# Feed-forward output product of a two-layer trunk on one core: 14 of 22 row blocks taken in pairs as 2x2 blocks with seven block products

## The chip, the cores and the metric

The kernel is one program on one core of a Trainium2 chip. The metric is the device time of one execution in microseconds (us). The engines named below are PE (the matrix engine), DVE (vector), ACT (scalar), POOL (general) and SP (which only issues DMAs here); each runs its own instructions in the order in which they stand in its queue and waits for semaphores of the others.

## The reference

Two layers; each has an attention part, a residual with layer norm, and a feed-forward part with the same residual and norm. SEQ is 512, D_MODEL 1024, D_FF 2816. The part that changes is the last matmul of `conv_ffn`:

```python
def conv_ffn(x, w_in, conv_w, conv_b, w_out):
    a, b = jnp.split(x @ w_in, 2, axis=-1)
    a = sum(conv_w[k] * a_pad[:, k:k + S] for k in range(CONV_W)) + conv_b
    return (jax.nn.gelu(a) * b) @ w_out
...
    ffn = conv_ffn(x, ffn_w_in[layer], ffn_conv_w[layer], ffn_conv_b[layer], ffn_w_out[layer])
    x = layer_norm(ALPHA * x + ffn, ln2_g[layer], ln2_b[layer])
```

All values are float32. The kernel holds each float32 operand as a high part `hi` (rounded by ACT to a narrower format that PE takes at full rate, fp32r) and a low part `lo` (the rest, by DVE), and makes each product as three matmuls: hi times hi, hi times lo, lo times hi.

## The kernel before

`layer0`, `ffn(0)`, `layer1`, `ffn(1)` run one after the other. The kernel's writer gives the instructions in program order; a list scheduler with a time model of its own then sets the order on each engine, so the order in the queues is not that of the source. Tiles come from pools with a fixed number of buffers: `raw` 5 (weights as loaded, 128x512), `hi` and `lo` 4 each (128x1024), `kj` 4 (128x1024), `kl` 2, `p` 4, `qq` 5 (128x512); a new tile of a pool waits until the last reader of a buffer is through.

The feed-forward part works on 22 blocks `f` of 128 hidden channels. Its input product makes, for each `f`, two sums `pa` (PSUM bank of tag `S`) and `pb` (tag `mm`), each 24 matmuls of 128x512 (`projT`: 8 slices of the model width by 3), with weights that `wab` loads, splits on ACT (L114) and DVE (L145) and hands over in `hi` and `lo`. `gate` (L592 to L598) applies the three-tap convolution and the gelu and writes `h[f]` (128 channels by 512 positions), by two ACT and three DVE instructions.

The output product sums over `f` into eight PSUM banks at once: four row tiles of 128 positions (`tb`) by two column halves of 512. `prep` splits `h[f]` into a `kj` tile and loads and splits the row block of `w_out`; `acc` then makes 4 x 2 x 3 = 24 matmuls of 128x512. So 528 matmuls a layer. The last blocks (TAIL: 5 in layer 0, 6 in layer 1) are all prepared first and then taken row tile by row tile, so that the first row tile's norm (`affine`, L540 to L565, mostly DVE) runs beside the products of the next. Each bank is added to the residual `nat[tb]` by one DVE instruction (L655). In layer 0 the norm is followed by transposes (L128) into the next layer's `xh`, `xl`; the memory keys and values of layer 1 (`mem_kv`) are placed there to fill PE.

## Time and profile before

| | us |
|---|---|
| median of 3 runs | 1282.38 (1282.27 to 1283.21) |
| span of the profiled execution | 1278.2 |
| median less that span | 4.2 |
| PE busy in the span | 1231.1 (96%) |
| DVE busy | 726.7 (57%) |
| ACT busy | 596.5 (47%) |
| POOL busy | 275.7 (22%) |

For the profiled execution the profile has the span, from its first instruction to its last, and no time of its own beside it; the runs' median lies 4.2 us above the span. A row of a group gives line, engine, operation, output from inputs, shape and count, then busy us, mean ns of one, and the idle time before it with what ended it. A row of the timeline gives start us, length us, engine, line, operation, shape and count. Matmuls are pipelined: the length of one (0.39 us) is longer than the distance between two starts. A line can be that of a helper: every matmul of the products stands at L120, and tiles tell them apart.

### The profile page before, as it was taken

How to read it: one execution, taken by the hardware profiler on the slowest of the kernel's cores; microseconds unless marked ns; L12 is line 12 of the kernel's file. 1: busy time of each engine (PE TensorE's matmuls, PEld its weight loads, DVE VectorE, ACT ScalarE, POOL GpSimd, SP SyncE). 2: the span in 40 equal slices, each digit the busy share in tenths (PEclk: the TensorE clock that was granted, in tenths of full speed). 3: DMA queues.
4: the chain of work that ended last, by engine and by line, in shares of the span. 5: the costliest groups of instructions: out<-in, count | busy, mean ns of one | idle time of the engine just before them, and what ended most of it. 6: DMA issues, size and time to landing. Idle time of an engine off the chain costs nothing.

```text
span 1278.2 us, 18386 instructions
## 1 busy us (share of the span) xinstructions
PE 1231.1 (96%) x6400; PEld 1048.4 (82%) x6400; DVE 726.7 (57%) x1605; ACT 596.5 (47%) x1271; POOL 275.7 (22%) x364
## 2 busy tenths in 40 slices
PE   7899999989999999999998999998999999999996
PEld 6788888879888888888888898886988888888885
DVE  5457787898544444433385665558854444443347
...
GB/s 230 218 201 75 42 34 58 48 127 83 120 95 99 99 99 99 98 89 95 131 42 124 67 78 89 74 100 140 35 131 99 99 92 93 97 99 99 99 74 66
DMA packets 164724, 125.94 MB, mean 99 GB/s; under 512 B 10743, under 2 KB 141175, under 8 KB 164632
## 3 DMA queue, kind: packets, MB, share of 16 engines
...
q14 instruction: 41, 0.34, 0.1%
...
## 4 chain that ended last, share of the span: by engine, by line
PE 82%; DVE 10%; DMA 3%; ACT 2%; issue 1%; POOL 0%; SPq 0%; DVEq 0%; ACTq 0%; POOLq 0%
PE psmm L120 40%; PE psS L120 27%; PE psPT L120 7%; PE psO L120 5%; PE psPT L128 3%; DVE pt L117 1%; DMA kj<-in_mem_dram 1%; DVE st L521 1%; DVE p L295 1%; DVE nat L553 1%; DVE nat L560 1%; DVE nat L505 1%; ACT p L300 1%; DVE xl L117 1%; ACT pt L114 1%
## 5 line engine op out<-in xcount | busy, mean ns | idle before, releaser
L114 ACT ACTIVATE hi<-raw 128x512 fp32r<-128x512 f32 x370 | 213.5, 622 | 274.2 <-PE psS L120 181.3
L145 DVE TENSOR_TENSOR lo<-raw,hi 128x512 fp32r<-128x512 f32 x294 | 192.0, 692 | 188.6 <-ACT hi L114 187.1
L120 PE MATMUL psmm<-xh,hi 128*128 128x512 f32 (+1 forms) x560 | 212.1, 379 | 0.0
L120 PE MATMUL psmm<-xh,lo 128*128 128x512 f32 (+1 forms) x560 | 211.9, 378 | 0.0
L120 PE MATMUL psmm<-xl,hi 128*128 128x512 f32 (+1 forms) x560 | 211.8, 378 | 0.0
L145 POOL TENSOR_TENSOR lo<-raw,hi 128x512 fp32r<-128x512 f32 x76 | 99.3, 1330 | 399.8 <-ACT hi L114 398.3
L120 PE MATMUL psS<-xh,hi 128*128 128x512 f32 (+1 forms) x408 | 151.3, 371 | 0.9 <-ACT G L750 0.9
L120 PE MATMUL psS<-xl,hi 128*128 128x512 f32 (+1 forms) x408 | 151.5, 371 | 0.1
L120 PE MATMUL psS<-xh,lo 128*128 128x512 f32 (+1 forms) x408 | 150.9, 370 | 0.0
L120 PE MATMUL psmm<-hi,kj 128*128 128x512 f32 x392 | 137.3, 400 | 4.2 <-ACT kj L114 3.2
L120 PEld LDWEIGHTS psmm<-xh,lo 128*128 128x128 f32 x560 | 105.5, 188 | 18.9
L120 PEld LDWEIGHTS psmm<-xh,hi 128*128 128x128 f32 x560 | 105.4, 188 | 18.8 <-DVE qq L248 0.2
L120 PEld LDWEIGHTS psmm<-xl,hi 128*128 128x128 f32 x560 | 105.3, 188 | 18.8
L551 POOL TENSOR_TENSOR nat<-nat,p 128x384 f32<-128x384 f32 (+2 forms) x16 | 20.5, 1283 | 360.9 <-issue 329.5
L304 POOL TENSOR_SCALAR p<-p,s 128x128 f32<-128x128 f32 (+3 forms) x144 | 74.7, 536 | 96.4 <-DVE s L271 49.1
L300 ACT ACTIVATE p<-p,s 128x128 f32<-128x128 f32 (+3 forms) x144 | 79.9, 556 | 33.0 <-DVE s L295 32.2
L120 PEld LDWEIGHTS psmm<-hi,kj 128*128 128x128 f32 x392 | 73.7, 189 | 19.4 <-ACT kj L114 3.5
L120 PEld LDWEIGHTS psS<-xh,hi 128*128 128x128 f32 x408 | 77.5, 190 | 14.0 <-ACT G L750 1.0
L120 PEld LDWEIGHTS psS<-xl,hi 128*128 128x128 f32 x408 | 77.4, 190 | 13.3 <-DVE xl L117 0.3
L120 PEld LDWEIGHTS psS<-xh,lo 128*128 128x128 f32 x408 | 77.4, 190 | 12.8
L120 PE MATMUL psPT<-hi,kj 128*128 128x512 f32 x228 | 81.7, 389 | 0.0
L295 DVE CUSTOM_DVE_ANT_0 p<-psS,T 128x128 f32<-128x128 f32 (+3 forms) x144 | 66.1, 484 | 23.1 <-PE psS L120 19.9
...
## 6 DMA issues: line engine op xcount, KB each, us to landing
raw<-in_ffn_w_in_dram SPq DMA_DIRECT2D x176, 256.0 KB, 3.1
raw<-in_ffn_w_out_dram SPq DMA_DIRECT2D x88, 256.0 KB, 3.0
...
raw<-in_shared_w_kv_dram SPq DMA_DIRECT2D x24, 256.0 KB, 3.0
raw<-in_a_w_out_dram SPq DMA_DIRECT2D x16, 256.0 KB, 2.9
raw<-in_b_w_in_dram SPq DMA_DIRECT2D x16, 256.0 KB, 3.1
raw<-in_b_w_out_dram SPq DMA_DIRECT2D x16, 256.0 KB, 3.2
raw<-in_a_w_in_dram SPq DMA_DIRECT2D x14, 256.0 KB, 3.9
```

The costliest lines, as they stand in the source:

```text
L114: self.nc.scalar.activation(dst, src, AF.Copy)
L117: self.nc.vector.tensor_sub(dst, src, hi.bitcast(F))
L120: self.nc.tensor.matmul(o, l, r, start=start, stop=stop)
L128: self.nc.tensor.transpose(o, i, self.ident)
L145: eng.tensor_sub(l[:, c], raw, h[:, c].bitcast(F))
L295: nc.vector.tensor_tensor_reduce(L[i], dst[i], T[:, 384 - 128 * i:512], op0=ALU.add, op1=ALU.min, scale=1.0, scalar=BIG, accum_out=nm[:, i ...
L300: nc.scalar.activation(L[i], L[i], AF.Exp, bias=nm[:, i:i + 1], scale=-1.0, accum_out=sm[:, i:i + 1])
L304: nc.gpsimd.tensor_scalar(L[i], L[i], r[:, i - qs[0]:i - qs[0] + 1], 1.0, op0=ALU.mult, op1=ALU.mult)
L505: nc.vector.scalar_tensor_tensor(self.nat[tb][:, sl], self.nat[tb][:, sl], ALPHA if first else 1.0, ps, op0=ALU.mult, op1=ALU.add)
L521: nc.vector.bn_stats(st[:, 6 * j:6 * j + 6], x[:, c0:c1])
L551: nc.gpsimd.tensor_mul(x[:, p], x[:, p], gt[:, p])
L553: nc.vector.scalar_tensor_tensor(x[:, d], x[:, d], mu, gt[:, d], op0=ALU.subtract, op1=ALU.mult)
```

## The change

Fourteen of the 22 blocks are taken in seven pairs. With the pair's two channel blocks split into position halves (a, c of the first; b, d of the second) and the two weight rows into column halves (v11, v12; v21, v22), the four output quarters need eight block products. The change makes seven of them, each 2 x 3 = 6 matmuls of 128x512 into two banks:

- `first`, made during the input product, while `pa` and `pb` of the other blocks go on: a times v11 into two banks `A`, and (c-a-d) times (v11+v12+v22) into two banks `B6`. `prepare` loads the four weight quarters into `raw`, makes the sums of weights on DVE and keeps them in tiles of `kj`, `p`, `kl`, `T`, `pc`, `ot` and `pt` that the input product does not use; it also overwrites the halves of `h` by their differences.
- `take_first`, once at the end of the input product: u = A + B6, added to or taken from six quarters of `nat`, which is scaled by ALPHA there.
- `second`: (a-c) times (v12+v22) into two banks `B7` (tag `S`), (c-d) times (v11+v12) into two banks `C5` (tag `mm`). No DMA; splits of 128x1024 and 128x512.
- `take_second`: four DVE instructions (L159) add B7 and C5 to `nat`. The banks then go on as part of the sums.
- `third`: b times v21 into `A`, (c-a-d+b) times v22 into `C5`, d times (v11+v12+v22+v21) into `B7`. The row of v21, v22 is loaded and split a second time. Two `kj` tiles per pair.

The other eight blocks go the old way, two or three of them between the pairs of `third`; the tail is as before. Per pair 42 matmuls take the place of 48. In the two programs PE has 5794 matmuls by the helper `mm` before and 5710 after, DVE 206 instructions more, ACT 74 more, SP 28 DMAs more.

```diff
--- before.py
+++ after.py
@@ -56,11 +56,125 @@
-YB = (("PT", "PT"), ("mm", "mm"), ("S", "S"), ("PT", "O"))
+NPAIR = 7
+KEEP_W = ("kj", "p", "p", "p", "p", "kl", "kl")
+KEEP_W4 = ("T", "T", "pc", "pc", "ot", "pt", "pt")
 HALVES = ((0, 512), (512, D))
+class Blocks:
+    def __init__(self, t, h, w):
+        self.t, self.h, self.w, self.k = t, h, w, {}
+        self.A = self.B6 = None
+    def raw(self, f, half):
+        r = self.t.al("raw")
+        self.t.nc.sync.dma_start(r, self.w[128 * f:128 * f + 128, 512 * half:512 * half + 512])
+        return r
+    def prepare(self, i):
+        t, nc = self.t, self.t.nc
+        h1, h2 = self.h[2 * i], self.h[2 * i + 1]
+        a, c, b, d = h1[:, 0:256], h1[:, 256:512], h2[:, 0:256], h2[:, 256:512]
+        ws = t.al(KEEP_W[i])
+        if KEEP_W[i] == "p":
+            s4 = ws[:, 1024:1280]
+        else:
+            if "s" not in self.k:
+                self.k["s"] = [t.al("kj"), 0]
+            n = self.k["s"][1]
+            s4 = self.k["s"][0][:, 256 * n:256 * n + 256]
+            self.k["s"][1] += 1
+        w4 = t.al(KEEP_W4[i])
+        v11, v12, v22, v21 = self.raw(2 * i, 0), self.raw(2 * i, 1), self.raw(2 * i + 1, 1), self.raw(2 * i + 1, 0)
+        w1, w3 = ws[:, 0:512], ws[:, 512:1024]
+        wh, wl = t.al("hi", R), t.al("lo", R)
+        t.hi(wh[:, 0:512], v11)
+        t.lo(wl[:, 0:512], v11, wh[:, 0:512])
+        nc.vector.tensor_add(w1, v11, v12)
+        nc.vector.tensor_add(w3, v12, v22)
+        nc.vector.tensor_add(w4, w1, v22)
+        t.hi(wh[:, 512:1024], w4)
+        t.lo(wl[:, 512:1024], w4, wh[:, 512:1024])
+        nc.vector.tensor_add(w4, w4, v21)
+        g = t.al("kj", R)
+        t.hi(g[:, 0:256], a)
+        t.lo(g[:, 512:768], a, g[:, 0:256])
+        nc.vector.tensor_sub(a, a, c)
+        nc.vector.scalar_tensor_tensor(s4, a, -1.0, d, op0=ALU.mult, op1=ALU.subtract)
+        nc.vector.tensor_sub(c, c, d)
+        t.hi(g[:, 256:512], s4)
+        t.lo(g[:, 768:1024], s4, g[:, 256:512])
+        nc.vector.tensor_add(s4, s4, b)
+        self.k[i] = ws, s4, w4
+        return g, wh, wl
+    def product(self, banks, lh, ll, rh, rl, start, stop, more=False):
+        for j in range(2):
+            c = slice(128 * j, 128 * j + 128)
+            self.t.mm3(banks[j], lh[:, c], ll[:, c], rh, rl, start, stop, more)
+    def first(self, i, e):
+        g, wh, wl = e
+        if self.A is None:
+            self.A, self.B6 = [self.t.ps("PT"), self.t.ps("PT")], [self.t.ps("PT"), self.t.ps("O")]
+        x = i == 0, i == NPAIR - 1
+        self.product(self.A, g[:, 0:256], g[:, 512:768], wh[:, 0:512], wl[:, 0:512], *x)
+        self.product(self.B6, g[:, 256:512], g[:, 768:1024], wh[:, 512:1024], wl[:, 512:1024], *x)
+    def take_first(self):
+        t, nc = self.t, self.t.nc
+        self.C5, self.B7 = [t.ps("mm"), t.ps("mm")], [t.ps("S"), t.ps("S")]
+        self.y = [[self.A[0], self.C5[0]], [self.A[1], self.C5[1]], [self.B7[0], self.B6[0]], [self.B7[1], self.B6[1]]]
+        for j in range(2):
+            u = t.al("qq")
+            nc.scalar.activation(u, self.A[j], AF.Copy)
+            nc.vector.tensor_add(u, u, self.B6[j])
+            for tb, c0, op in ((j, 512, ALU.subtract), (2 + j, 0, ALU.add), (2 + j, 512, ALU.subtract)):
+                x = t.nat[tb][:, c0:c0 + 512]
+                nc.vector.scalar_tensor_tensor(x, x, ALPHA, u, op0=ALU.mult, op1=op)
+    def second(self, i):
+        t = self.t
+        ws, h1 = self.k[i][0], self.h[2 * i]
+        g, wh, wl = t.al("kj", R), t.al("hi", R), t.al("lo", R)
+        t.hi(g[:, 0:512], h1)
+        t.lo(g[:, 512:1024], h1, g[:, 0:512])
+        t.hi(wh, ws[:, 0:1024])
+        t.lo(wl, ws[:, 0:1024], wh)
+        x = i == 0, i == NPAIR - 1
+        self.product(self.B7, g[:, 0:256], g[:, 512:768], wh[:, 512:1024], wl[:, 512:1024], *x)
+        self.product(self.C5, g[:, 256:512], g[:, 768:1024], wh[:, 0:512], wl[:, 0:512], *x)
+    def take_second(self):
+        for bank, op in ((self.B7, ALU.subtract), (self.C5, ALU.add)):
+            for j in range(2):
+                x = self.t.nat[2 + j][:, 512:1024]
+                self.t.nc.vector.tensor_tensor(x, x, bank[j], op=op)
+    def third(self, i):
+        t = self.t
+        _, s4, w4 = self.k[i]
+        h2 = self.h[2 * i + 1]
+        g = t.al("kj", R)
+        t.hi(g[:, 0:512], h2)
+        t.lo(g[:, 512:1024], h2, g[:, 0:512])
+        v = t.rows(self.w, 256 * i + 128)
+        q = t.al("qq", R)
+        t.hi(q[:, 0:256], s4)
+        t.lo(q[:, 256:512], s4, q[:, 0:256])
+        w = t.al("kj", R)
+        t.hi(w[:, 0:512], w4)
+        t.lo(w[:, 512:1024], w4, w[:, 0:512])
+        self.product(self.A, g[:, 0:256], g[:, 512:768], v[0][:, 0:512], v[1][:, 0:512], False, False, True)
+        self.product(self.C5, q[:, 0:256], q[:, 256:512], v[0][:, 512:1024], v[1][:, 512:1024], False, False, True)
+        self.product(self.B7, g[:, 256:512], g[:, 768:1024], w[:, 0:512], w[:, 512:1024], False, False, True)
 class Trunk:
@@ -116,13 +230,13 @@
-    def mm(self, o, l, r, start, stop):
-        self.nc.tensor.matmul(o, l, r, start=start, stop=stop)
-    def mm3(self, o, lh, ll, rh, rl, start, stop):
-        self.mm(o, lh, rh, start, False)
-        self.mm(o, lh, rl, False, False)
-        self.mm(o, ll, rh, False, stop)
+    def mm(self, o, l, r, start, stop, more=False):
+        self.nc.tensor.matmul(o, l, r, start=start, stop=stop, skip_group_check=more)
+    def mm3(self, o, lh, ll, rh, rl, start, stop, more=False):
+        self.mm(o, lh, rh, start, False, more)
+        self.mm(o, lh, rl, False, False, more)
+        self.mm(o, ll, rh, False, stop, more)
@@ -602,6 +716,7 @@
         w = [wab(f) for f in range(2)]
         self.los = (nc.vector,)
+        blocks = Blocks(self, h, wout)
         p = [(self.ps("S"), self.ps("mm")) for f in range(2)]
@@ -611,15 +726,20 @@
             gate(f, *p[f])
         for f in range(2, NF):
             wa, wb = wab(f)
+            pair = f // 2 - 1 if f % 2 == 0 and f // 2 - 1 < NPAIR else None
+            if pair is not None:
+                e = blocks.prepare(pair)
             pa, pb = self.ps("S"), self.ps("mm")
             self.projT(pa, wa)
             self.projT(pb, wb)
             gate(f, pa, pb)
-        gt, bt = self.gb(a["ln2_g"], a["ln2_b"], l)
-        y = [[self.ps(t) for t in ts] for ts in YB]
-        if not last:
-            self.new_xT()
+            if pair is not None:
+                blocks.first(pair, e)
+        blocks.take_first()
+        for i in range(NPAIR):
+            blocks.second(i)
+        blocks.take_second()
+        y = blocks.y
         def prep(f, store=None, tag="kj"):
             t = self.al(tag, R)
@@ -631,14 +751,27 @@
             sl = slice(128 * tb, 128 * tb + 128)
             for c0, c1 in cols:
                 c = slice(c0, c1)
+                own = tb >= 2 and c0 == 512
                 self.mm3(y[tb][c0 // 512][:, c0 % 512:c0 % 512 + c1 - c0], hh[:, sl], hl[:, sl], w[0][:, c], w[1][:, c],
-                         f == 0, f == NF - 1)
+                         f == 2 * NPAIR and own, f == NF - 1, not own)
         TAIL, nx, nv = (6, 4, 0) if last else (5, 0, 2)
-        for f in range(NF - TAIL):
+        plain = list(range(2 * NPAIR, NF - TAIL))
+        for i in range(NPAIR):
+            blocks.third(i)
+            if plain and i % 2 == 1:
+                f = plain.pop(0)
+                e = prep(f)
+                for tb in range(NT):
+                    acc(f, tb, *e)
+        for f in plain:
             e = prep(f)
-            for tb in (1, 0, 2, 3) if f == 0 else range(NT):
+            for tb in range(NT):
                 acc(f, tb, *e)
+        gt, bt = self.gb(a["ln2_g"], a["ln2_b"], l)
+        if not last:
+            self.new_xT()
+        TAIL, nx, nv = (6, 4, 0) if last else (5, 0, 2)
         stores = [None] * (TAIL - nv - nx)
@@ -652,7 +785,7 @@
                 for f in range(NF - TAIL, NF):
                     acc(f, tb, *es[f - NF + TAIL], ((c0, c1),))
                 c = slice(c0, c1)
-                nc.vector.scalar_tensor_tensor(self.nat[tb][:, c], self.nat[tb][:, c], ALPHA,
+                nc.vector.scalar_tensor_tensor(self.nat[tb][:, c], self.nat[tb][:, c], ALPHA if tb < 2 and c0 == 0 else 1.0,
                                                y[tb][c0 // 512][:, c0 % 512:c0 % 512 + c1 - c0], op0=ALU.mult, op1=ALU.add)
```

Where it moves instructions, the rows of the queues show it. The first place is DVE at the end of layer 0's input product. Before: `psS_5615` and `psmm_5616` are the two sums of the last block, `lo_...` are splits of the output weights.

```order
L145 TENSOR_TENSOR lo_5763<-raw_5764,hi_5762 128x512
L145 TENSOR_TENSOR lo_5763<-raw_5768,hi_5762 128x512
L593 SCALAR_TENSOR_TENSOR qq_5665<-psS_5615,cw,qq_5665 128x511
L595 SCALAR_TENSOR_TENSOR qq_5665<-psS_5615,cw,qq_5665 128x510
L598 TENSOR_TENSOR pt_3902<-qq_5665,psmm_5616 128x512
L145 TENSOR_TENSOR lo_5800<-raw_5801,hi_5799 128x512
L145 TENSOR_TENSOR lo_5800<-raw_5805,hi_5799 128x512
L117 TENSOR_TENSOR kl_6366<-pt_3902,kl_6366 128x512
L117 TENSOR_TENSOR kj_5833<-o_3896,kj_5833 128x512
L145 TENSOR_TENSOR lo_5837<-raw_5838,hi_5836 128x512
```

After: `psS_5907` and `psmm_5908` are the two sums of the last block, `psPT_4259` and `psO_4260` the banks of B6, `qq_5967` and `qq_5973` hold u, `nat_129` to `nat_132` are the four row tiles, `lo_6038` is the split of a kept weight sum of the fourth pair.

```order
L707 SCALAR_TENSOR_TENSOR qq_5957<-psS_5907,cw,qq_5957 128x511
L138 TENSOR_TENSOR qq_5967<-qq_5967,psPT_4259 128x512
L138 TENSOR_TENSOR qq_5973<-qq_5973,psO_4260 128x512
L231 TENSOR_TENSOR qq_6129<-kj_4172,qq_6129 128x256
L709 SCALAR_TENSOR_TENSOR qq_5957<-psS_5907,cw,qq_5957 128x510
L231 TENSOR_TENSOR qq_6166<-p_4369,qq_6166 128x256
L141 SCALAR_TENSOR_TENSOR nat_129<-nat_129,qq_5967 128x512
L141 SCALAR_TENSOR_TENSOR nat_131<-nat_131,qq_5967 128x512 x2
L141 SCALAR_TENSOR_TENSOR nat_130<-nat_130,qq_5973 128x512
L141 SCALAR_TENSOR_TENSOR nat_132<-nat_132,qq_5973 128x512 x2
L231 TENSOR_TENSOR lo_6038<-p_4755,hi_6037 128x1024
L712 TENSOR_TENSOR pt_3902<-qq_5957,psmm_5908 128x512
```

Between the two convolution steps and the product of the last gate stand now the additions of `take_first` and one wide split; before, the three of the gate stood together.

The second place is PE in the output product of layer 0. Before, the end of the second block (`kj_5722` is its split channel block) is like every other: three matmuls a bank, bank after bank.

```order
L120 MATMUL psS_5679<-hi_5725,kj_5722 128x512
L120 MATMUL psS_5679<-lo_5726,kj_5722 128x512
L120 MATMUL psS_5679<-hi_5725,kj_5722 128x512
L120 MATMUL psS_5680<-hi_5725,kj_5722 128x512
L120 MATMUL psS_5680<-lo_5726,kj_5722 128x512
L120 MATMUL psS_5680<-hi_5725,kj_5722 128x512
L120 MATMUL psPT_5681<-hi_5725,kj_5722 128x512
L120 MATMUL psPT_5681<-lo_5726,kj_5722 128x512
L120 MATMUL psPT_5681<-hi_5725,kj_5722 128x512
L120 MATMUL psO_5682<-hi_5725,kj_5722 128x512
```

After, at the start of `third`: `kj_6116` and `kj_6153` are the channel blocks of the first two pairs, `kj_6132` the summed weights of the first, `psPT_4257` and `psPT_4258` the banks A, `psS_5965` and `psS_5966` the banks B7, `psmm_5963` one of C5.

```order
L234 MATMUL psPT_4258<-hi_6119,kj_6116 128x512
L234 MATMUL psPT_4257<-hi_6156,kj_6153 128x512
L234 MATMUL psPT_4257<-lo_6157,kj_6153 128x512
L234 MATMUL psPT_4258<-hi_6156,kj_6153 128x512
L234 MATMUL psPT_4258<-lo_6157,kj_6153 128x512
L234 MATMUL psS_5965<-kj_6132,kj_6116 128x512 x3
L234 MATMUL psS_5966<-kj_6132,kj_6116 128x512 x3
L234 MATMUL psPT_4257<-hi_6156,kj_6153 128x512
L234 MATMUL psPT_4258<-hi_6156,kj_6153 128x512
L234 MATMUL psmm_5963<-hi_6119,qq_6129 128x512
```

The scheduler has mixed the products of neighbouring pairs, and the bank of C5 comes only after 18 matmuls of other banks.

The third place is DVE at the end of layer 0, in the norm of the last row tile (`nat_132`); `kj_...` are splits of the memory keys and values, `xl_...` of the next layer's input. Before:

```order
L531 TENSOR_SCALAR s_1252_6833<-s_1252_6833 128x1
L533 SCALAR_TENSOR_TENSOR s_1253_6834<-s_1252_6833,s_1254_6835 128x1
L534 SCALAR_TENSOR_TENSOR s_1253_6834<-s_1253_6834 128x1
L145 TENSOR_TENSOR lo_6995<-raw_6996,hi_6994 128x512
L535 SCALAR_TENSOR_TENSOR s_1252_6833<-s_1253_6834,s_1252_6833 128x1
L145 TENSOR_TENSOR lo_6995<-raw_7000,hi_6994 128x512
L536 SCALAR_TENSOR_TENSOR s_1253_6834<-s_1252_6833,s_1254_6835 128x1
L117 TENSOR_TENSOR kj_6571<-psmm_6592,kj_6571 128x4x64
L537 SCALAR_TENSOR_TENSOR s_1252_6833<-s_1253_6834,s_1252_6833 128x1
L560 SCALAR_TENSOR_TENSOR nat_132<-nat_132,s_1252_6833,p_5672 128x512
L560 SCALAR_TENSOR_TENSOR nat_132<-nat_132,s_1252_6833,p_5672 128x128
L117 TENSOR_TENSOR kj_6571<-psmm_6592,kj_6571 128x4x64
```

After:

```order
L645 TENSOR_SCALAR s_1318_7011<-s_1318_7011 128x1
L231 TENSOR_TENSOR kj_6740<-psmm_6715,kj_6740 64x256
L647 SCALAR_TENSOR_TENSOR s_1319_7012<-s_1318_7011,s_1320_7013 128x1
L648 SCALAR_TENSOR_TENSOR s_1319_7012<-s_1319_7012 128x1
L649 SCALAR_TENSOR_TENSOR s_1318_7011<-s_1319_7012,s_1318_7011 128x1
L650 SCALAR_TENSOR_TENSOR s_1319_7012<-s_1318_7011,s_1320_7013 128x1
L651 SCALAR_TENSOR_TENSOR s_1318_7011<-s_1319_7012,s_1318_7011 128x1
L674 SCALAR_TENSOR_TENSOR nat_132<-nat_132,s_1318_7011,p_6487 128x512
L674 SCALAR_TENSOR_TENSOR nat_132<-nat_132,s_1318_7011,p_6487 128x128
L231 TENSOR_TENSOR kj_6740<-psmm_6715,kj_6740 64x256
L231 TENSOR_TENSOR xl_6491<-psPT_6962,xh_6490 128x4x128
L259 TENSOR_TENSOR lo_7055<-raw_7056,hi_7054 128x512
```

Before, two weight splits (`lo_6995`) stand between the steps of the reciprocal root (L533 to L537) and ahead of the last step of the norm (L560), for which the last transposes wait. After, that chain (L647 to L651, then L674) stands together but for one small split, and the next weight split (`lo_7055`) stands behind it.

## The prediction

> **What bounds the kernel now.** The first view is the page: PE is busy for nearly the whole span, and the chain that ended last is PE for 82% of it.
>
> ```profile
> PE 1231.1 (96%) x6400; PEld 1048.4 (82%) x6400; DVE 726.7 (57%) x1605; ACT 596.5 (47%) x1271; POOL 275.7 (22%) x364
> PE 82%; DVE 10%; DMA 3%; ACT 2%; issue 1%; POOL 0%; SPq 0%; DVEq 0%; ACTq 0%; POOLq 0%
> ```
>
> The share is an average, so the feed-forward stretches are read by themselves, in the view of windows: input product and output product of layer 0, then of layer 1. The columns after the stretch are its length, then busy us of PE, weight load, DVE, ACT, POOL, the granted clock, the DMA share and GB/s.
>
> ```profile
> 460.00:520.00 60.00, 60.00 (x266) 49.70 (x265) 25.30 (x39) 19.83 (x33) 0.00 (x0) 1.00 0.33 98
> 560.00:600.00 40.00, 40.00 (x178) 33.14 (x177) 13.91 (x23) 13.04 (x24) 0.00 (x0) 1.00 0.30 95
> 1000.00:1060.00 60.00, 60.00 (x266) 49.70 (x265) 25.68 (x39) 20.39 (x34) 0.00 (x0) 1.00 0.34 99
> 1160.00:1200.00 40.00, 40.00 (x178) 33.10 (x178) 14.97 (x24) 12.97 (x24) 0.00 (x0) 1.00 0.30 93
> ```
>
> In all four PE never stops and its clock is whole; DVE is busy for 35 to 43%, ACT for 32 to 34%, POOL not at all. So here a matmul less is its distance less, as long as DVE and ACT keep up. The distance is in the timeline: one start in the input product and the start 48 matmuls later, then the same in the output product, 24 matmuls apart.
>
> ```profile
> 500.58 0.39 PE L120 MATMUL psmm<-xh,hi 128*128 128x512 f32 x1
> 511.46 0.39 PE L120 MATMUL psmm<-xh,hi 128*128 128x512 f32 x1
> 571.30 0.39 PE L120 MATMUL psPT<-hi,kj 128*128 128x512 f32 x1
> 576.74 0.39 PE L120 MATMUL psPT<-hi,kj 128*128 128x512 f32 x1
> ```
>
> 10.88 us over 48 and 5.44 us over 24 are both 0.2267 us a matmul.
>
> **Matmuls removed.** A pair takes 42 matmuls for 48; 7 pairs in 2 layers make 84 fewer, which is also what the two programs' counts say (5794 and 5710). 84 x 0.2267 = 19.0 us, all of it on the path. The Trainium skill ("TensorE: Matmul & The Clock Gate", Back-to-back issue gap) gives about 131 ns for a 512-column matmul in a sustained stream of loads and matmuls; by that it would be 84 x 0.131 = 11.0 us. The trace has 227 ns and decides.
>
> **Splits and sums added, in the input product.** The prices are the group rows of the same operations.
>
> ```profile
> L114 ACT ACTIVATE hi<-raw 128x512 fp32r<-128x512 f32 x370 | 213.5, 622 | 274.2 <-PE psS L120 181.3 <-PE psmm L120 69.8 <-issue 10.0
> L145 DVE TENSOR_TENSOR lo<-raw,hi 128x512 fp32r<-128x512 f32 x294 | 192.0, 692 | 188.6 <-ACT hi L114 187.1 <-ACT p L377 1.1
> L593 DVE SCALAR_TENSOR_TENSOR qq<-psS,cw,qq 128x511 f32<-128x511 f32 x44 | 32.7, 744 | 0.0
> L117 DVE TENSOR_TENSOR pt<-psPT,pt 128x256 fp32r<-128x256 f32 x24 | 10.0, 417 | 1.3 <-ACT pt L114 1.2
> L114 ACT ACTIVATE hi<-kj 128x1024 fp32r<-128x1024 f32 x1 | 1.1, 1057 | 1.7 <-DMA kj<-in_a_w_in_dram 1.7
> ```
>
> `prepare` is six DVE operations of 512 columns and six of 256: 6 x 0.69 + 6 x 0.42 = 6.7 us a pair. Two blocks' ordinary work on DVE is 8 splits and two gates, 8 x 0.69 + 2 x (2 x 0.744 + 0.69) = 9.9 us. Together 16.6 us, against PE's 2 x 10.88 + 12 x 0.2267 = 24.5 us: 68%, covered. ACT has less. I charge nothing. If the cover went, it would be for lack of buffers: a pair puts a fifth tile beside the four of `hi`, and four quarters into the ring of five `raw` tiles. Walked with these rows, in the order of the queues, the weights of each block are split at least 8 us before PE wants them (the second half of a block's weights, for one, waits for the tile that PE leaves 13 us before their use). The DMAs added, 2 x 28 quarters of 256 KB less 2 x 14 that `third` no longer loads, lift the input product from 98 GB/s to 12 x 256 KB in 24.5 us, 128 GB/s; the first slices of the program move more, and SP has nothing else queued there but the same ring:
>
> ```profile
> GB/s 230 218 201 75 42 34 58 48 127 83 120 95 99 99 99 99 98 89 95 131 42 124 67 78 89 74 100 140 35 131 99 99 92 93 97 99 99 99 74 66
> ```
>
> **The handover.** At the end of the input product PE needs eight banks again. Seven are free early. The bank of the last `pb` is free only after the last gate's product, and in the order on DVE that product now stands behind `take_first` and a wide split (first place in the section on the change). Consecutive operations overlap a little, as two rows of the timeline show:
>
> ```profile
> 566.60 1.14 ACT L114 ACTIVATE hi<-raw 128x512 fp32r<-128x512 f32 x2
> 567.33 1.29 DVE L145 TENSOR_TENSOR lo<-raw,hi 128x512 fp32r<-128x512 f32 x2
> ```
>
> so in a full queue ACT takes 0.52 and DVE 0.60 us apiece, 0.09 to 0.10 less than the single length. Let T be the end of the last input matmul. The half before ended 5.44 us earlier; ACT then splits 1024 columns and starts the gate, and DVE follows with a 1024-column split (no such row on DVE: 0.69 + 2 x (0.69 - 0.42) = 1.23 us, an estimate from the 256 and 512 rows) until T - 3.0. Then 0.66 (convolution), 1.20 (u), 0.33, 0.66, 0.33, 3.60 (six quarters), 1.14 (split), 0.69 (product): T + 5.6. PE has 27 matmuls for other banks first in its order, until T + 27 x 0.2267 = T + 6.1. So no wait, by half a us; without any overlap DVE would be at T + 6.9, a wait of 0.8. I take 0.3 a layer, between 0 and 0.8. `second` itself needs 1.23 + 0.69 on DVE and 1.06 + 0.62 on ACT per pair against 12 x 0.2267 = 2.72 on PE, and three pairs are split ahead of T. On SP the norm's factors and layer 1's memory rows now wait for `p` tiles, which the kept sums free by T + 10; a weight load queued behind them is due at T + 17 and gets its own `raw` tile only at T + 14, so this costs nothing.
>
> **The turn to the third products.** `take_second` must read C5 before PE goes on in it. PE reaches it after 84 + 18 matmuls (second place), T + 23.1. On DVE the tiles that the fifth and sixth pair leave set the pace: the summed weights of `third` go into a tile that PE leaves at T + 16.5; after ACT (0.63) DVE has seven operations, 7 x 0.60, and the read, 0.69: T + 22.5 at best, T + 23.6 without overlap. 0.3 a layer, between 0 and 0.9 with a margin like that of the handover.
>
> **`third`.** Per pair DVE has four operations of 512 and one of 256, 3.2 us, ACT as many, 2.9 us, PE 18 x 0.2267 = 4.1 us. Covered on average; but each pair takes two of four `kj` tiles where a block took one, so a split can wait for PE's last reader. One exposed turn costs the last matmul's length, ACT and DVE: 0.39 + 0.63 + 0.69 = 1.7 us. Walked through, the tiles come round in time because other products stand between. I take 0.3 a layer, between 0 and two exposed turns, 3.4.
>
> **End of layer 0 and after.** PE waits there once for long, and the clock falls. The waits of PE after layer 0's output product, and three windows (columns as above):
>
> ```profile
> PE psPT L128 <- DVE nat L560: 3.7, 1, 3.7
> PE psmm L120 <- ACT kj L114: 3.0, 1, 3.0
> PE psO L120 <- DVE o L280: 2.7, 3, 2.0
> ```
>
> ```profile
> 680.00:684.00 4.00, 2.51 (x14) 2.38 (x15) 2.99 (x8) 1.76 (x4) 1.12 (x2) 0.79 0.68 201
> 684.00:688.00 4.00, 4.00 (x29) 4.00 (x29) 0.43 (x1) 0.39 (x1) 0.00 (x0) 0.79 0.00 0
> 635.00:680.00 45.00, 42.72 (x264) 37.75 (x262) 38.25 (x91) 20.35 (x40) 24.52 (x22) 1.00 0.26 77
> ```
>
> The chain of the last norm is in DVE's timeline, and in the chain that ended last for the end of layer 1:
>
> ```profile
> 675.51 0.22 DVE L533 SCALAR_TENSOR_TENSOR s<-s,s 128x1 f32<-128x1 f32 x1
> 680.68 1.01 DVE L560 SCALAR_TENSOR_TENSOR nat<-nat,s,p 128x512 f32<-128x512 f32 x2
> ...
> 1271.33 1.00 DVE s L533
> 1273.19 0.75 DVE nat L560
> ```
>
> From 638 to 681 the norms on DVE set the end (38 of 45 us busy), not PE. In the new order two splits leave the last norm's chain (third place): there it takes 680.68 - 675.51 = 5.2 us, at the end of layer 1, where nothing stands in it, 1273.19 - 1271.33 = 1.9, so up to 3.3 us can go. Against that PE has the memory products earlier and fewer left for that wait: if all of the 3.3 us were lost the other way, it would be as much more. The scheduler has also set layer 1's attention anew; the waits of 3.0 and 2.7 us lie there and may close or be joined by others like them. I take 0, between -5 and +4, for both.
>
> **The sum.** 1278.2 - 19.0 + 2 x (0.3 + 0.3 + 0.3) = 1261.0 us of span; the runs' median lies 4.2 us above the span, so **1265.0 us**. The unknowns reach from -1.8 - 5 to +8.4 + 4.
>
> **Rivals.**
> - *Splits come late.* The `kj` tiles expose every second pair of `third` and the handovers cost their upper bounds: 7 x 1.7 + 2 x 1.7 = 15.3 us back, 1278.6. For it: DVE and ACT work in step with PE's releases already (the group row of L145: 187 us of idle time ended by ACT). Against: the walk.
> - *The weights of the input product come late* (slower). Four of five `raw` tiles wait for the sums of a pair, so the next block's weights are loaded, split on ACT and split on DVE with nothing ahead. The page has 3.1 us to land:
>
> ```profile
> raw<-in_ffn_w_in_dram SPq DMA_DIRECT2D x176, 256.0 KB, 3.1
> ```
>
> ```profile
> SPq L142 <- DVE lo L145: 51.5, 25, 4.4
> ```
>
>   3.1 + 0.62 + 0.69 = 4.4 us for each of 14 pairs, 61.7 us, less 19.0: 1325. It decides from 19.0 / 14 = 1.4 us a pair. For it: SP already waits on DVE for free `raw` tiles in the output product (second row). Against: 8 us of lead.
> - *The clock falls in the mixed passes* (slower). The second and third products change the bank at almost every matmul. Were each change a short stop that the clock answers with 0.79, as above, the 210 matmuls of these passes in each layer, 47.6 us, would take 47.6 / 0.79, 12.7 us more, 25.3 in all: 1290. It decides below 95.2 / (95.2 + 19.0) = 0.83. Against: the output product changes the bank at every third matmul at 1.00. The Trainium skill (same page, A second HAM failure mode: psum-queue depth-cycling) says that cycling through banks at 512 columns can make the clock swing.
> - *More than the matmuls.* The end of layer 0 gives its 3.3 us and the 1.7 us of clock (8 us at 0.79): 1258 to 1260.
> - That the matmuls are not saved is ruled out by the counts.
>
> **Chances.** Forecast 0.70 (1260 to 1270), late splits 0.15 (1270 to 1282), late weights 0.03, clock 0.03, more 0.09 (1256 to 1260). The range 1259 to 1273 leaves out most of the last three and the far half of the late splits. A measurement of this kernel tells about 0.2%, 2.6 us, from no change. Faster: 0.70 + 0.09 + 0.12 of the late splits = 0.91; same 0.03; slower 0.06.
>
> **What would show it.** In the profile of the changed kernel: matmul starts 0.2267 us apart through both feed-forward parts; stretches of the input product with PE at its full length; in PE's waits nothing above 1 us on the gate's product (L712), on L159 or on `kj` splits; clock 1.00 in the second and third products; the norm of layer 0's last row tile followed by a wait of no more than 3.7 us. The prediction is wrong if the input product has gaps, if PE waits several times for `kj` splits, or if the distance of matmuls grows where banks change.

## The result and the profile after

The changed kernel takes 1268.28 us (median of 4 runs, 1266.39 to 1268.47), the kernel before in the same session 1282.8 us (4 runs, 1282.27 to 1285.32). The ratio is 0.9882, 95% interval 0.9868 to 0.9897: 14.5 us less in the medians, where 17.4 were forecast (1265.0, range 1259 to 1273). The profiled execution of the changed kernel has a span of 1266.5 us, 11.7 less than the one of before, where the sum said 1261.0.

From the page, the engines PE, DVE and ACT and the chain that ended last:

```profile
PE 1215.7 (96%) x6316; PEld 1033.3 (82%) x6316; DVE 839.6 (66%) x1811; ACT 635.9 (50%) x1345; POOL 276.1 (22%) x364
PE 81%; DVE 10%; ACT 3%; DMA 2%; issue 2%; SPq 1%; POOL 0%; DVEq 0%; ACTq 0%; POOLq 0%
```

PE has lost 15.4 us of busy time, DVE has gained 113. Whether DVE's gain is hidden is read from the windows (stretch, its length, busy PE, weight load, DVE, ACT, POOL, clock, DMA share, GB/s): input product of layer 0, then its second passes, its third passes, then input product and third passes of layer 1.

```profile
400.00:460.00 60.00, 60.00 (x267) 49.69 (x266) 35.66 (x62) 22.65 (x41) 0.00 (x0) 1.00 0.41 125
562.00:590.00 28.00, 28.00 (x125) 23.21 (x124) 22.54 (x36) 15.84 (x29) 0.00 (x0) 1.00 0.51 159
590.00:630.00 40.00, 40.00 (x178) 33.11 (x178) 24.45 (x38) 21.35 (x38) 2.55 (x2) 1.00 0.50 158
1000.00:1060.00 60.00, 60.00 (x266) 49.71 (x265) 36.01 (x63) 22.49 (x40) 0.00 (x0) 1.00 0.43 127
1190.00:1245.00 55.00, 55.00 (x245) 45.52 (x244) 35.41 (x68) 25.00 (x43) 5.73 (x4) 1.00 0.27 86
```

PE is full and its clock whole in all five, with DVE at 59% in the input product (43% was the most before) and 80% in the second passes. So the loss is elsewhere. To find it, both spans are cut at five instructions that both kernels have: the first gate of layer 0, its last input matmul, the first gate of layer 1, its last input matmul, and the last matmul of all. In the timeline of the kernel before (start, duration, engine, line):

```profile
315.93 0.76 ACT L592 ACTIVATE qq<-psS,cb,cw 128x512 f32<-128x512 f32 x1
538.43 0.39 PE L120 MATMUL psmm<-xh,lo 128*128 128x512 f32 x1
925.03 0.76 ACT L592 ACTIVATE qq<-psS,cb,cw 128x512 f32<-128x512 f32 x1
1148.25 0.39 PE L120 MATMUL psmm<-xh,lo 128*128 128x512 f32 x1
1267.93 0.39 PE L120 MATMUL psO<-xh,kl 128*128 128x512 f32 x1
```

and in that of the changed kernel:

```profile
318.13 0.76 ACT L706 ACTIVATE qq<-psS,cb,cw 128x512 f32<-128x512 f32 x1
559.67 0.39 PE L234 MATMUL psmm<-xh,lo 128*128 128x512 f32 x1
921.84 0.76 ACT L706 ACTIVATE qq<-psS,cb,cw 128x512 f32<-128x512 f32 x1
1164.10 0.39 PE L234 MATMUL psmm<-xh,lo 128*128 128x512 f32 x1
1255.87 0.39 PE L234 MATMUL psO<-xh,kl 128*128 128x512 f32 x1
```

| stretch | before | after | difference | by matmuls x 0.2267 | lost |
|---|---|---|---|---|---|
| opening and layer 0's attention, to its first gate | 315.93 | 318.13 | +2.20 | 0 | 2.20 |
| to the last input matmul, layer 0 | 222.50 | 241.54 | +19.04 | 84: +19.04 | 0 |
| output product, norms, layer 1's attention, to its first gate | 386.60 | 362.17 | -24.43 | -126: -28.56 | 4.13 |
| to the last input matmul, layer 1 | 223.22 | 242.26 | +19.04 | 84: +19.04 | 0 |
| output product of layer 1, to the last matmul | 119.68 | 91.77 | -27.91 | -126: -28.56 | 0.65 |
| last norm, to the end of the span | 10.27 | 10.63 | +0.36 | 0 | 0.36 |

The differences sum to -11.7. The feed-forward products give what their matmuls are worth to a hundredth, but for 0.65 us in layer 1. That is one place, seen in the timelines of ACT and PE (in square brackets the idle time ahead, and what ended it):

```profile
1187.20 0.63 ACT L228 ACTIVATE kj<-T 128x512 fp32r<-128x512 f32 x1 [1.95 <-PE psS L234]
1187.88 0.74 PE L234 MATMUL psS<-kj,kj 128*128 128x512 f32 x2 [0.27 <-ACT kj L228]
```

A split for `third` waits until PE has left the `kj` tile, and PE then waits for that split: the exposed turn that the prediction describes, once and in part. (The 0.27 goes by the modelled end of a matmul; by the distances of the starts in that place it is 0.6.)

The largest loss, 4.1 us, lies for its larger part at the end of layer 0. PE's waits from 640 to 690 us, and two windows:

```profile
PE psPT L242 <- DVE nat L674: 2.7, 3, 1.4
PE psmm L234 <- DVE kj L231: 1.1, 1, 1.1
PE psmm L234 <- POOL lo L259: 0.7, 1, 0.7
PE psPT L242 <- POOL nat L677: 0.3, 1, 0.3
```

```profile
660.00:670.00 10.00, 6.85 (x47) 5.73 (x46) 9.59 (x22) 6.46 (x13) 9.79 (x9) 0.91 0.38 115
670.00:680.00 10.00, 8.90 (x56) 8.73 (x55) 5.69 (x8) 3.73 (x8) 5.88 (x6) 0.75 0.40 113
```

Before, there was one wait of 3.7 us, and 8 us at 0.79 cost 1.7 us of full clock, 5.4 in all. Now the waits make 4.8 us, and the clock costs 10 x 0.09 + 10 x 0.25 = 3.4, 8.2 in all, 2.8 more. That counts clock which was missing while PE waited. With the whole stretch cut into windows of 1 us, and the clock counted only where PE is busy, it divides so:

| PE in the stretch to layer 1's first gate | before | after | difference |
|---|---|---|---|
| idle | 11.1 | 12.2 | +1.1 |
| clock missing while busy | 4.5 | 5.8 | +1.4 |
| the rest, work at full clock | 371.0 | 344.1 | -26.9 (126 matmuls: -28.6) |

So 2.4 of the 4.1 us are waits and clock, and they lie ahead of 690 us: behind it, in layer 1's attention, both together make 10.1 before and 10.0 after. The other 1.7 us are neither. They repeat in the later profiles (370.6 to 371.0 with the old feed-forward part in layer 0, 343.9 to 344.6 with the new one of seven pairs); where they lie stays open.

Why PE waits is in its order. The last product ahead of the wait and the last row tile's transposes before, then these transposes and the next of memory's products after:

```profile
677.49 0.28 PE L120 MATMUL psmm<-hi,xl 128*128 128x256 f32 x1
681.49 0.77 PE L128 MATMUL psPT<-ident,nat 128*128 128x128 f32 x5 [3.73 <-DVE nat L560]
```

```profile
667.46 0.66 PE L242 MATMUL psPT<-ident,nat 128*128 128x128 f32 x4 [1.40 <-DVE nat L674]
669.64 0.41 PE L234 MATMUL psmm<-lo,o 128*128 128x256 f32 x1
```

Before, all 96 of memory's products (those with a tile `o`) and 24 of layer 1's own had run by then. After, 29 of memory's 96 stand behind these transposes in PE's order, where they cannot fill its wait. Whether they could have run sooner the trace does not say: POOL makes low parts of weights up to 668.5 us, and PE waits 0.7 us for one. And the last norm itself gained little. Its last operation on DVE, and POOL beside it:

```profile
665.75 2.93 DVE L674 SCALAR_TENSOR_TENSOR nat<-nat,s,p 128x512 f32<-128x512 f32 x2
665.59 2.95 POOL L259 TENSOR_TENSOR lo<-raw,hi 128x512 fp32r<-128x512 f32 x2
```

From the reciprocal root (663.59 us) to this operation the chain takes 2.2 us where it took 5.2, as the order promised. But the operation lies beside two POOL splits now and takes 2.93 us, where it took 1.01 with POOL nearly idle. From the start of the last addition (659.03 us, before 671.30) to the end of the norm it is 9.6 us, before 10.4.

### The profile page after: what moved, and what is told of

It reads as the page before. It is cut to its first block, busy times and chain, and to the rows that moved or that the text cites. A ratio compares the mean times of both kernels' runs of the same rounds, so it can differ in the third digit from the quotient of the medians.

```text
span 1266.5 us, 18512 instructions
## 1 busy us (share of the span) xinstructions
PE 1215.7 (96%) x6316; PEld 1033.3 (82%) x6316; DVE 839.6 (66%) x1811; ACT 635.9 (50%) x1345; POOL 276.1 (22%) x364
## 4 chain that ended last, share of the span: by engine, by line
PE 81%; DVE 10%; ACT 3%; DMA 2%; issue 2%; SPq 1%; POOL 0%; DVEq 0%; ACTq 0%; POOLq 0%
PE psmm L234 40%; PE psS L234 27%; PE psPT L234 6%; PE psO L234 4%; PE psPT L242 3%; DVE pt L231 1%; DVE nat L674 1%; DVE p L409 1%; DVE st L635 1%; ACT p L414 1%; DMA kj<-in_mem_dram 1%; ACT hi L228 1%; DVE nat L667 1%; DVE nat L619 1%; DMA raw<-in_a_cmp_w_v_dram 1%
## 5 line engine op out<-in xcount | busy, mean ns | idle before, releaser
L228 ACT ACTIVATE hi<-raw 128x512 fp32r<-128x512 f32 x356 | 206.8, 623 | 276.1 <-PE psS L234 145.8
L259 DVE TENSOR_TENSOR lo<-raw,hi 128x512 fp32r<-128x512 f32 x266 | 180.8, 712 | 119.1 <-ACT hi L228 118.3
L234 PE MATMUL psmm<-hi,kj 128*128 128x512 f32 x336 | 118.4, 401 | 2.1 <-ACT kj L228 1.7
L231 DVE TENSOR_TENSOR pt<-psPT,pt 128x512 fp32r<-128x512 f32 (+2 forms) x124 | 73.5, 604 | 10.1 <-ACT pt L228 9.4
L228 ACT ACTIVATE pt<-psPT 128x512 fp32r<-128x512 f32 (+2 forms) x124 | 63.9, 530 | 25.9 <-PE psPT L242 18.1
```

The lines of the kernel that those rows point to most:

```text
L228: self.nc.scalar.activation(dst, src, AF.Copy)
L231: self.nc.vector.tensor_sub(dst, src, hi.bitcast(F))
L234: self.nc.tensor.matmul(o, l, r, start=start, stop=stop, skip_group_check=more)
L259: eng.tensor_sub(l[:, c], raw, h[:, c].bitcast(F))
```

## The experiments

**e1: the kernel before, profiled again.** No edit. The question is whether the 2.2 us in the opening belong to the change.

> The kernel before, profiled a second time. The two profiles differ already ahead of the change: the first gate's activation of layer 0 starts at 315.93 us before and at 318.13 us after, with the same orders on all engines up to there. Theory A (the opening varies between executions): this profile's first gate lies anywhere between 315 and 319 us, and span and time of this execution differ by the 1.8 us that the four runs after show (1268.28 - 1266.5), so the profiled execution of before was a quick one, some 2 us under its median. Theory B (the changed program is slower in the opening): 315.9 us again, within 0.3.

Measured: 1282.21 us with a span of 1280.3, 1.9 apart, and the first gate of layer 0 at

```profile
318.69 0.76 ACT L592 ACTIVATE qq<-psS,cb,cw 128x512 f32<-128x512 f32 x1
```

Theory A holds. The rest of the span repeats: 222.50, 385.99, 223.22 and 119.69 us for the table's four stretches. The opening varies between executions (315.9 to 320.3 us in the profiles of this study up to that gate), the stretches by at most 0.9, so from here on stretches are compared and whole times only where the loss is larger than 2 us.

**e2 and e3: the pairs in one layer alone.** A copy of the old feed-forward method is put beside the new one and called for one layer; for e2:

```diff
-        self.ffn(0, False)
+        self.ffn_plain(0, False)
```

and for e3 the same with `self.ffn(1, True)`. The order on every engine is that of before up to layer 1's feed-forward part in e2, and that of the changed kernel up to there in e3.

> Pairs in layer 1 alone, layer 0 as before. Theory A (the feed-forward parts give nearly all that the matmuls are worth, and the miss is in layer 0's end and layer 1's attention): 42 x 0.2267 = 9.5 us less, minus the 0.65 that layer 1's output product and the 0.4 that the last norm lose in the profile after: 8.5 us below before, 8.0 to 9.5. Theory B (each layer's handover, turn and third products cost the same, and the whole miss of some 5 us is theirs): 9.5 - 2.5 = 7.0 us below. Both profiles' order up to layer 1's feed-forward part is that of before, so layer 0's end must show one wait of PE of about 3.7 us.

> Pairs in layer 0 alone, layer 1's feed-forward part as before. Theory A: 9.5 us less, minus about 3 us at the end of layer 0 and 1.2 in layer 1's attention: 5.3 us below before, 4.5 to 6.0. Theory B: 7.0 us below. With the layer-1 kernel it should add up to the whole change, 13.8 to 14.5 us.

Measured: e2 1272.73 us (1271.48 to 1274.61; before 1282.13), ratio 0.9927, 0.9914 to 0.9940, 7.7 to 11.0 us less; e3 1277.35 us (1274.33 to 1279.42), ratio 0.9964, 0.9951 to 0.9978, 2.8 to 6.3 us less. Theory B's 7.0 lies outside both intervals, and the two medians add to 14.2 us, nearly the whole change of 14.5. The stretches say it sharper. Layer 1's output product in e2, and layer 0's last input matmul and layer 1's first gate in e3:

```profile
1170.66 0.39 PE L235 MATMUL psmm<-xh,lo 128*128 128x512 f32 x1
1262.43 0.39 PE L235 MATMUL psO<-xh,kl 128*128 128x512 f32 x1
```

```profile
561.86 0.39 PE L235 MATMUL psmm<-xh,lo 128*128 128x512 f32 x1
924.39 0.76 ACT L814 ACTIVATE qq<-psS,cb,cw 128x512 f32<-128x512 f32 x1
```

91.77 us again (the 0.65 repeat), and 362.53 us (4.5 lost): the 4.1 belong to layer 0's new feed-forward part, through what follows it.

**e4: four pairs in place of seven.**

```diff
-NPAIR = 7
+NPAIR = 4
```

> Four pairs in each layer in place of seven: 48 matmuls fewer than before, 36 more than after. Theory A (the loss comes once, with the new order of banks at layer 0's end, and no pair costs anything by itself): 36 x 0.2267 = 8.2 us above after, 6.3 us below before. Theory B (the loss is in proportion to the pairs): 4/7 of the gain of after, 8.3 us below before, 6.2 above after.

Measured: 1272.95 us (1270.27 to 1274.08), ratio 0.9926, 0.9914 to 0.9939, 9.5 us less: above both numbers, nearer to B's. The stretches from layer 0's last input matmul and from layer 1's:

```profile
551.05 0.39 PE L234 MATMUL psmm<-xh,lo 128*128 128x512 f32 x1
924.65 0.76 ACT L706 ACTIVATE qq<-psS,cb,cw 128x512 f32<-128x512 f32 x1
1158.76 0.39 PE L234 MATMUL psmm<-xh,lo 128*128 128x512 f32 x1
1262.12 0.39 PE L234 MATMUL psO<-xh,kl 128*128 128x512 f32 x1
```

373.60 us is 13.0 less than before where 72 matmuls are worth 16.3: 3.3 lost. 103.36 is 16.32 less: nothing lost. The 3.3 lie between the 4.1 that A keeps whole and the 2.4 of B's proportion, 0.8 and 0.9 from them, and the same stretch varies by as much in kernels of one order: this run does not decide between the two. Layer 1's exposed turn does not come with four pairs. A's number was too low since it counted all small losses; by the stretches this kernel gains 10.9 - 3.3 = 7.6, a little under the 7.8 to 11.0 of the whole times, which hold the opening's spread besides.

**e5, e6, e7: other orders at the end of layer 0.** Three one-line edits: memory's transposes go to the S banks (e5), memory's work is issued behind the third row tile's norm (e6), the tail has six row blocks (e7).

```diff
-                    self.mem2 = self.mem_kv(a["b_w_mem_kv"][0], "mm", "p")
+                    self.mem2 = self.mem_kv(a["b_w_mem_kv"][0], "S", "p")
```

```diff
-                if tb == 0:
+                if tb == 2:
                     self.los, self.proj_tags = (nc.gpsimd,), ("mm",)
```

```diff
-        TAIL, nx, nv = (6, 4, 0) if last else (5, 0, 2)
+        TAIL, nx, nv = (6, 4, 0) if last else (6, 0, 2)
```

> The changed kernel, with layer 1's memory rows transposed into the S banks in place of the mm banks (one argument). In the changed kernel the mm banks come free with the additions at 633.1 and 637.6 us, the S banks only with those at 643.5 and 654.4 us, so memory's products come behind the last feed-forward products and the norms' chain on DVE. The stretch to compare goes from the last input matmul of layer 0 to the first gate of layer 1: 386.6, 386.0 and 386.8 us in the profiles with the old feed-forward part in layer 0, 362.2 and 362.5 with the new, where 126 matmuls less would give 358.1. Theory A (the new bank order starts memory's work inside the norms' chain, so that PE runs out of it before the last norm ends: waits of 4.9 us and 6.8 us at half clock in place of 3.7 and 3.4): 358 to 360 us, and 2 to 4 us less in all than the changed kernel. Theory B (the four norms on DVE need their time whatever stands beside them; the loss is that the feed-forward products, shorter now, no longer cover them): 362 us as it is, within 0.7.

> The changed kernel, with layer 1's memory work issued behind the norm of the third row tile in place of the first; its transposes still go to the mm banks. In the order on PE the last feed-forward products stand ahead of memory's first product, but memory's transposes and their splits on DVE still lie among them. Theory A (memory inside the norms' chain is the cost): between the changed kernel and the kernel that moves the banks: 359 to 361.5 us for the same stretch. Theory B: 362 us, within 0.7.

> The changed kernel, with six row blocks in place of five in layer 0's tail, so that the first addition comes 24 - 3 = 21 matmuls, 4.8 us, further ahead of the last product. Theory B (the norms on DVE need their time): the chain starts 4.8 us earlier against PE, its last wait goes, 358 us for the stretch. Theory A: memory still lies in the chain, so most of the loss stays: 360 to 362; and the sixth block's hi and lo tiles are held to the end, so that memory's weights get theirs later, which could make it up to 3 us worse than now.

Measured: e5 1275.18 us, ratio 0.9941 (0.9925 to 0.9957), the stretch 370.27; e6 1268.09 us, 0.9876 (0.9857 to 0.9896), the stretch 361.56; e7 1268.57 us, 0.9887 (0.9871 to 0.9904), the stretch 362.19. Theory A fell with e5, and so did B, which gave 362 there: memory later makes it 8.1 us slower. PE's waits there, 640 to 690 us, and the two windows with the lowest clock:

```profile
PE psPT L242 <- DVE nat L674: 4.0, 1, 4.0
PE psPT L242 <- POOL nat L677: 2.9, 1, 2.9
PE psmm L234 <- DVE kj L231: 2.1, 2, 1.4
PE psS L242 <- DVE o L231: 0.7, 1, 0.7
```

```profile
660.00:670.00 10.00, 9.22 (x57) 8.98 (x55) 6.63 (x21) 4.26 (x9) 3.09 (x4) 0.72 0.09 27
670.00:680.00 10.00, 6.50 (x33) 6.18 (x34) 4.56 (x7) 4.25 (x10) 3.97 (x6) 0.66 0.37 107
```

9.7 us of waits where the changed kernel has 4.8: memory's products stand behind the transposes that wait for the norms, and on an engine that works in order they can't fill those waits. Theory B's 358 us in e7 failed as well: the chain starts earlier, and PE still waits, once for 4.9 us. e6 can't be told from the changed kernel. None of the three is a repair.

**e8 and e10: the sums made several times over.** The first three sums of a pair are repeated, 4 times in e8 and 9 times in e10.

```diff
-        nc.vector.tensor_add(w1, v11, v12)
-        nc.vector.tensor_add(w3, v12, v22)
-        nc.vector.tensor_add(w4, w1, v22)
+        for _ in range(4):
+            nc.vector.tensor_add(w1, v11, v12)
+            nc.vector.tensor_add(w3, v12, v22)
+            nc.vector.tensor_add(w4, w1, v22)
```

> The changed kernel, with the first three sums of each pair (512 columns) made four times over, nine DVE operations more a pair, same values. In the changed kernel's input product DVE is busy 35.7 of 60 us, 14.6 of a pair's 24.5 us; nine more at 0.60 to 0.69 us are 5.4 to 6.2 us, so 20 to 21 of 24.5. Theory A (the sums are covered by PE's matmuls): the stretch from the first gate of layer 0 to the last input matmul stays 241.5 us, within 0.5, and layer 1's 242.3. Theory B (the sums sit in a chain with the splits of the next weights, whose lead is 8 us): late weights, 7 pairs x (5.8 - what is left of the lead), up to some 10 us more a layer.

> The changed kernel, with the first three sums of each pair made nine times over: 24 more DVE operations a pair than in the changed kernel, same values. With nine more the stretch stayed at 241.54 us. Now DVE has 14.6 + 24 x 0.60 to 0.69 = 29.0 to 31.2 us for a pair where PE has 24.5 us, so the cover must be gone: 4.5 to 6.7 us for each of 7 pairs, 272 to 288 us from the first gate of layer 0 to its last input matmul. If the lead of the weights (8 us) hides a part once, 265 to 272. If the time stayed below 250, DVE's share of time would not say where the cover ends.

Measured: e8 1267.44 us, the input products 241.54 and 242.27; e10 1367.06 us, 288.32 and 292.90. The window of layer 0's input product in e8, then in e10:

```profile
400.00:460.00 60.00, 60.00 (x267) 49.69 (x266) 51.80 (x90) 25.57 (x47) 0.00 (x0) 1.00 0.48 144
```

```profile
400.00:460.00 60.00, 52.60 (x208) 38.80 (x207) 55.47 (x95) 17.92 (x31) 0.00 (x0) 0.97 0.34 103
```

DVE at 86% (e8) costs PE nothing, so B fell. In e10 a pair's DVE work by single lengths, 14.6 + 24 x 0.69 = 31.2 us, passes PE's 24.5, and each pair costs (288.32 - 241.54) / 7 = 6.7 us, the difference; in layer 1 it is 7.2. DVE is busy for 92% of that window, not all of it, and PE's waits in layer 0's input product (345 to 600 us) are mostly for ACT's weight splits, 25.9 of 28.6 us: the overload reaches PE as late weights. Somewhere between the two runs the cover ends; where, no run shows.

**e11: one `raw` tile less.** A fifth tile is held from the start of each input product to its end, so a pair's quarters fill the other four.

```diff
         self.A = self.B6 = None
+        self.held = t.al("raw")
+        t.nc.gpsimd.memset(self.held, 0.0)
...
             nc.vector.tensor_add(u, u, self.B6[j])
+            if j == 0:
+                nc.vector.tensor_add(u[:, 0:1], u[:, 0:1], self.held[:, 0:1])
```

> The changed kernel, with one of the five raw tiles filled with zeros at the start of each layer's input product and read once at its end (one element, plus zero), so that four are left for the weights there and a pair's quarters take them all. Theory A (a lead of about 8 us): a quarter less of the ring costs about one load, 3 us, of the lead: 241.5 us within 1. The rival of the prediction, late weights: 4.4 us for each of 7 pairs, 272 us. Anything between says how much of the lead the fifth tile carries.

Measured: 1268.22 us, the input products 241.54 and 242.26, PE full:

```profile
400.00:460.00 60.00, 60.00 (x266) 49.69 (x266) 36.39 (x63) 23.47 (x42) 0.00 (x0) 1.00 0.42 126
```

The rival of late weights has nothing left for this kernel: even with one tile fewer nothing is late.

**e9: work put into PE's wait.**

```diff
+                if tb == NT - 1:
+                    x = self.ps("S")
+                    for _ in range(16):
+                        self.mm(x, es[4][0][:, 0:128], es[4][2][0][:, 0:512], True, True)
```

> The changed kernel, and behind layer 0's last feed-forward products 16 more matmuls of 512 columns whose result nobody reads, into a free S bank: 16 x 0.2267 = 3.6 us of work for PE in the place where it waits 4.9 us for the last norms and then runs 6.8 us at half clock. In the order on PE nine stand behind the last feed-forward product, two ahead of the third tile's last transposes, five ahead of the last tile's. Theory C (the half clock is the price of PE's waits there): waits shorter by about 3 us, the half clock gone or halved, and so 1.7 to 3.4 us less: 359 to 360.5 us from the last input matmul of layer 0 to the first gate of layer 1 (362.2 now, 361.6 to 363.1 in the five profiles with the changed order). Theory D (the clock falls for something else in that stretch, its short products or transposes): half clock as now, 362 us, and up to 3.6 us more if the matmuls stand in the way.

Measured: 1273.21 us, ratio 0.9926 (0.9913 to 0.9940), the stretch 367.00: 4.8 worse than the changed kernel, beyond D's bound of 3.6. C fell as it was put: all 16 ran before the last norm was near its end, and one wait of 3.8 us stood behind them, with the same clock loss by the window, 10 x 0.34 = 3.4 us. So the wait was not filled, and whether the half clock goes with it stays untested here:

```profile
PE psPT L242 <- DVE nat L674: 3.8, 1, 3.8
```

```profile
670.00:680.00 10.00, 7.68 (x42) 7.42 (x43) 5.55 (x9) 4.38 (x10) 4.69 (x6) 0.66 0.45 131
```

This trace shows why the last norm comes so late, 12.1 us from the start of the last addition to its end. DVE's timeline in that place, then POOL's:

```profile
666.35 0.69 DVE L231 TENSOR_TENSOR xl<-psPT,xh 128x512 fp32r<-128x512 f32 x1
666.95 1.19 DVE L649 SCALAR_TENSOR_TENSOR s<-s,s 128x1 f32<-128x1 f32 x1
668.18 1.19 DVE L650 SCALAR_TENSOR_TENSOR s<-s,s 128x1 f32<-128x1 f32 x1
```

```profile
666.83 2.52 POOL L259 TENSOR_TENSOR lo<-raw,hi 128x512 fp32r<-128x512 f32 x2
```

Operations of one column, which take 0.15 to 0.25 us elsewhere, last about as long as one of the two POOL splits beside them (1.26).

**e12: those POOL splits left out.** The kernel leaves out the low parts of layer 1's memory weights, so its output is not the reference's; the hi parts stand in their place, and PE's work is the same. Of the eight splits two ran at 623 us in the changed kernel, the others from 655.4 us on.

```diff
-        h, l = store or (self.al("hi", R), self.al("lo", R))
+        h = self.al("hi", R) if self.hi_only else None
+        h, l = (h, h) if h is not None else store or (self.al("hi", R), self.al("lo", R))
...
-            eng.tensor_sub(l[:, c], raw, h[:, c].bitcast(F))
+            if not self.hi_only:
+                eng.tensor_sub(l[:, c], raw, h[:, c].bitcast(F))
...
+                    self.hi_only = True
                     self.mem2 = self.mem_kv(a["b_w_mem_kv"][0], "mm", "p")
+                    self.hi_only = False
```

> The changed kernel without the low parts of layer 1's memory weights (their hi tile stands for lo in the products, so PE's work is the same): eight 512-column splits fewer on POOL, which lie at 655 to 677 us, beside the last norms. In all profiles of this kernel the norm's one-column operations on DVE take 0.15 to 0.25 us where POOL is idle, and up to 1.19 to 1.22 us where one of these splits runs (1.25 to 1.30 us each): 0.99 at 655.74 and 1.19 at 663.86 in the changed kernel, five in a row in the kernel with the filled wait. Theory E (POOL's splits hold up the norms' chain on DVE, and that sets the end of layer 0): no one-column operation above 0.5 us there, the last norm's final operation 1 to 2 us sooner after the last addition than the 6.7 us now, and 360 to 361 us from the last input matmul of layer 0 to the first gate of layer 1. Theory F (the chain is set by the sum of DVE's own work and the half clock follows): 362.2 to 363.1 us as in the five profiles with this order.

Measured: 1263.48 us (1261.97 to 1263.83; before 1283.15), ratio 0.9842 (0.9824 to 0.9859), the stretch 355.79: 6.4 less than the changed kernel. PE's waits from 640 to 690 us and the two windows:

```profile
PE psmm L235 <- DVE kj L232: 1.0, 2, 0.6
```

```profile
660.00:670.00 10.00, 9.81 (x82) 9.40 (x80) 9.48 (x24) 9.39 (x21) 8.15 (x7) 1.00 0.67 201
670.00:680.00 10.00, 9.15 (x75) 9.01 (x76) 5.45 (x9) 3.16 (x7) 4.19 (x4) 1.00 0.45 130
```

Waits 1.0 for 4.8, clock loss 0 for 3.4 (3.2 while PE is busy): 7.0 to 7.2 us, against 6.4 of the stretch; the work at full clock stays, 344.0. F fell, and E's 360 to 361 was too high. E is wrong on the way as well: from the start of the last addition to the norm's last operation it is 8.6 us (659.64 to 668.25) for 6.7, to its end 9.6 for 9.6, and three one-column operations, beside the two splits and the norm's product that remain on POOL, still take 0.61 to 0.94. What changed on PE is that memory's products no longer wait for low parts (that was the 0.7 in the list above), and its order: all 96 run ahead of the last tile's transposes, the last 48 of them from 663.09 us on without a wait:

```profile
669.05 0.77 PE L243 MATMUL psPT<-ident,nat 128*128 128x128 f32 x5
```

So it is shown that without these eight splits, and with the order that comes of it, the waits and the lost clock at the end of layer 0 go. It is not shown that the splits are what the change made worse: the kernel before has POOL splits there too, and was not run without them, and 355.79 us is 2.3 below what the matmuls alone would give (386.60 - 28.56), so part of the 6.4 was never this change's loss. How much goes through DVE's stretched operations and how much through PE's order stays open as well; the norm that takes as long as before speaks for the order.

## Why the prediction was right, and by how much its terms were off

- **What bounds it, and the matmuls.** Right to a hundredth: each input product has 84 matmuls more and takes 19.04 us more, 84 x 0.2267; with four pairs (e4) layer 1's output product has 72 fewer and takes 16.32 less, 72 x 0.2267. The Trainium skill ("TensorE: Matmul & The Clock Gate", Back-to-back issue gap) with its 131 ns would have made the change 8 us too small; these runs have 226.7 ns throughout.
- **Splits and sums at nothing.** Right. e8 shows that nine more operations a pair would have been hidden too, e10 that 24 more are not, e11 that the lead of the weights was ample. The sum counted 16.6 us of DVE a pair; the trace has 14.6.
- **Handover, turn and `third`: 1.8 us.** Measured 0 in layer 0 (no wait of PE from 560 to 640 us) and 0.65 in layer 1, in the place and by the mechanism of the term on `third`. The handover and the read of C5 cost nothing, as their walks said; the 0.3 added to each was not needed.
- **End of layer 0 and after: 0, between -5 and +4.** This is the step that was mis-sized: 4.1 us in the profile after and 4.5 in e3 (386.60 - 362.53 = 24.07 of 28.56), just past its upper end. The prediction named both sides, the norm's chain freed of two splits and memory's products used up earlier, and let them cancel. The chain did lose 3.0 of the 3.3 us that it could, but not because of the splits alone, which are 1.4 of its 5.2 us before: three one-column operations beside POOL took 0.87 to 1.23 there. POOL's work then took 1.9 back from the norm's last operation. On the other side memory's products were not used up: 29 of them stood behind the wait in PE's order. In all the waits grew by 1.1, the clock's price by 1.4, and 1.7 is not found. How waits and clock share the price is partly chance: in e11, whose order there is much the same, the waits are 5.4 and the clock 1.7, with the stretch 0.6 longer. The named test, a wait of no more than 3.7 us, holds for the longest (1.4) and misses the point: their sum grew.
- **From span to median: 4.2 us.** Right in size, for a reason that the prediction could not see. Span and time of one execution differ by 1.8 (1266.5 and 1268.28); the other 2.4 were a quick opening in the profiled execution of before. (The last addition is rounded down: 1261.0 + 4.2 is 1265.2.) With 1282.4 - 19.0 + 4.1 + 0.65 + 0.36 the medians close: 1268.5, measured 1268.3. The 1.15 us that the term above charged too much hid part of the 4.1.
- **The last norm** took 0.36 more; the sum had no term for it.
- **The rivals.** Late splits: one turn, 0.65 us. Late weights: e11. The clock in the mixed passes: 1.00 in their windows, with PE full but for the 0.65; the order rows ahead of the prediction show a change of bank at every second matmul (7 among 14), not at almost every one. The swing that the Trainium skill ("TensorE: Matmul & The Clock Gate", A second HAM failure mode: psum-queue depth-cycling) describes, which it puts down to frequent short idle times of PE between groups of matmuls, does not come here, where PE is full. More than the matmuls: the end of layer 0 went the other way.
